# Up-projection weights asked for a chunk ahead, and a transition in which GpSimd keeps the program's order

## The chip, the cores and the metric

The kernel runs on one core of one Trainium2 chip. The metric is the device time of one execution in microseconds (us). A core has five engines that run programs of their own and meet at semaphores: TensorE (PE in the profile; matmuls, results in PSUM), VectorE (DVE), ScalarE (ACT), GpSimd (POOL) and SyncE (SP). SP issues nearly all transfers (DMAs) here, in the order of its program: one that waits for its source holds back those behind it.

## The reference

One decoder layer on x of 1024 tokens by 1024 features, in float32:

```python
h = rmsnorm(x, g_mix) * (1 + sc_m) + sh_m
x = x + gt_m * dsa_mixer(h, ...)            # indexer, top 256 keys, attention on a shared latent
h = rmsnorm(x, g_ffn) * (1 + sc_f) + sh_f
u, v = split(h @ f_w_in, 2)                 # 1024 -> 2 x 2816
u = causal_depthwise_conv(u, f_conv_w, width=3) + f_conv_b
x = x + gt_f * ((gelu(u) * v) @ f_w_out)    # 2816 -> 1024
return rmsnorm(x, g_final)
```

The shifts, scales and gates (`sh`, `sc`, `gt`) are linear in silu(c).

## The kernel before

Every large product is made at float32 accuracy from two parts per operand: a high part (a cast to the matmul format, on ScalarE) and a low part (operand minus its high part, on VectorE or GpSimd). Each 128-deep step is three matmuls of 128x512: high by high, high by low, low by high (`three`). A product with four steps is twelve matmuls.

*The up-projection.* f_w_in is cut into NF = 22 chunks of 128 columns of u and of v. For each chunk `c` the 2x2 block product (u and v by two halves of the tokens) is made with seven products `m0` to `m6` instead of eight, Strassen's way. Their token-side operands (`s3`, `s4`, `b11`, `b22` in `comb`, and `s1`, `s7`, `s6`) are sums of blocks of the normalised tokens `hm`, made once. Their weight-side operands are made for each chunk: two loads, `fw{c}_1` (the v columns) and `fw{c}_0` (the u columns), 512 KB each; for some products a sum of two blocks into `ring` on GpSimd (`prep_sum`); then the high part of `pr{c}_{i}` on ScalarE and its low part on GpSimd, for product 3 on VectorE (`prep_split`). After a product, `after` evicts it: `v` and `u` are put together by VectorE and ScalarE; when m5 is in, ScalarE's `conv` activation starts the convolution, VectorE's two taps follow, then the GELU, and VectorE multiplies with v (`gate`). The result goes to memory (`ga<-conv`); for every second chunk, four sums of two chunks' results (`sa`, `sb`) go there as well.

*Output weights.* The down-projection uses sums of blocks of f_w_out as well. For each pair q of chunks, `w_sums(q)` loads two tiles `wb`, makes four sums and one product with the gate on VectorE and stores them (`wt`). Seven pairs are done in the attention's last part; the remaining four fall into the up-projection, one each in the time of chunks 4, 8, 12 and 16.

*Order.* `LEAD` = 2: when a product is issued, sums are made for products up to two or three ahead and parts for two ahead. Loads follow a plan: (step, chunk) pairs from `LOAD_AT`, where step 7c + `LOAD_AT[j]` asks for `fw{c+1}`. Chunks 0 and 1 are loaded by hand. A scheduler orders each engine's instructions by estimated times, except for engines in the set `in_order`, which keep the program's order.

*The transition.* The loop over r finishes the tokens tile by tile: the output projection `w1` (into `wo`, added to the residual `xr`), the norm (`ss`, `rx`, `rxr`, `xn`), the transposes (`xt`) and `hm` in `w2a`, the parts for `comb` in `w2b`, the pair sums of tiles o and 4 + o in `w2c` (three operations on `hm`), and the parts of `s1`, `s7` and `s6` in `w2d`. Behind the loop, the code for tile 7 is written out by hand together with the first products of chunks 0 and 1, with VectorE, ScalarE and TensorE in program order (`in_order |= set("PAD")`). After the last `w2d` the set is cleared, and the loop over `seq` does the rest.

Of the kernel before, what the change touches and what calls it, by code (L numbers as in the profile page):

```python
# [15 lines left out]
OP = mybir.AluOpType  # L16

T, D, P = 1024, 1024, 128
NT, KD = T // P, D // P
# [45 lines left out]
NW = 'PDDDPPDD'  # L65
W2B_DVE = {(6, 1), (4, 1), (5, 1), (6, 0), (7, 0), (7, 1)}
HM_ACT = (3, 6, 7)
LOAD_AT = (3, 3)
UP_LOW_DVE = ((3,), (3, 6))
D_ORDER = (1, 2, 5, 6, 3, 7, 4)  # L70
D_LOAD, D_SPLIT = 16.0, 7.0
# [5 lines left out]
def body(ctx, tc, a):  # L77
    nc = tc.nc
    in_order = set("PADG")
# [19 lines left out]
    pe, act, dve, pool = [Engine(e, n) for e, n in zip((nc.tensor, nc.scalar, nc.vector, nc.gpsimd), "PADG")]  # L99
# [11 lines left out]
    def slot(shape, dt, name):  # L111
        return slots.tile(shape, dt, name=name, tag="slot")
# [4 lines left out]
    def bank1(name):  # L117
        return bank2(name)[:, :512]
# [4 lines left out]
    def cyc(n, name, bufs, dt=F):  # L123
        return const.tile([P, n], dt, name=name, tag=name, bufs=bufs)

    def split(dst_h, dst_l, src, low):
        act.copy(dst_h, src)
        low.tensor_tensor(dst_l, src, dst_h.bitcast(F), op=OP.subtract)

    def three(out, lh, ll, rh, rl, first, last):  # L130
        pe.matmul(out, lh, rh, start=first, stop=False)
        pe.matmul(out, lh, rl, start=False, stop=False)
        pe.matmul(out, ll, rh, start=False, stop=last)
# [81 lines left out]
    def rstd(ss, n, width, name):  # L215
        t = cyc(width, name, 4)
        dve.tensor_scalar(t, ss, 1.0 / n, EPS, op0=OP.mult, op1=OP.add)
        r = cyc(width, name + "r", 4)
        pool.tensor_tensor(r, t, mhalf.to_broadcast([P, width]), op=OP.pow)
        return r  # L220
# [844 lines left out]
    ost, xn1 = {}, {}  # L1065
# [5 lines left out]
    def w0(t):  # L1071
        if t == 0:
            load_xr(0)
        if t + 1 < NT:
            load_xr(t + 1)
        pt = bank2("ot")
        for k in range(KD):
            pe.transpose(pt[:, k * P:(k + 1) * P], o_sb[t][:, k], ident)
        o_h = slot([P, KD, P], R, "o_h")
        o_l = slot([P, KD, P], R, "o_l")  # L1080
        ost[t] = o_h, o_l
        split(o_h, o_l, pt.rearrange("p (k t) -> p k t", k=KD), dve)

    def w1(t, between=None):

        o_h, o_l = ost[t]
        if between:
            halves = [bank1("wo") for _ in range(2)]
        else:
            ps = bank2("wo")  # L1090
            halves = [ps[:, :512], ps[:, 512:]]
        x1 = x_r[t]
        for j in range(2):
            js = slice(j * 512, (j + 1) * 512)
            for k in range(KD):
                three(halves[j], o_h[:, k], o_l[:, k], wo[k][0][:, js], wo[k][1][:, js], k == 0, k == KD - 1)
            if between:
                dve.tensor_tensor(x1[:, js], halves[j], x1[:, js], op=OP.add)
                if j == 0:
                    between()  # L1100
        if between is None:
            dve.tensor_tensor(x1, ps, x1, op=OP.add)
            nc.sync.dma_start(x1d[t], x1)
            xn1[t] = norm(x1, NW[t])
# [12 lines left out]
    def w2a(t, halves):  # L1117

        hf, o = divmod(t, 4)
        hm[t] = g = slot([P, KD, P], F, f"hm{t}")  # L1120
        for k in range(KD):
            pe.transpose(halves[k // 4][:, k % 4], xn1[t][:, k * P:(k + 1) * P], ident)
        if t in HM_ACT:
            on_dve = 4 if t >= NT - 2 else 0
            if on_dve:
                dve.tensor_tensor(g[:, 0:4], halves[0], bc(ada["a_f"][:, 0:4]), op=OP.mult)
                dve.tensor_tensor(g[:, 0:4], g[:, 0:4], bc(sh_f[:, 0:4]), op=OP.add)
            for k in range(on_dve, KD):
                act.activation(g[:, k], halves[k // 4][:, k % 4], AF.Identity, bias=sh_f[:, k:k + 1], scale=a_f[:, k:k + 1])
        else:  # L1130
            for i in range(2):
                ks = slice(4 * i, 4 * i + 4)
                dve.tensor_tensor(g[:, ks], halves[i], bc(ada["a_f"][:, ks]), op=OP.mult)
            dve.tensor_tensor(g, g, bc(sh_f), op=OP.add)
# [20 lines left out]
    def load_up(c, j):  # L1155
        raw[c, j] = w = slot([P, 2, 4, P], F, f"fw{c}_{j}")
        nc.sync.dma_start(w, a["f_w_in"][c, :, j].rearrange("p (h k m) -> p h k m", h=2, k=4))
# [17 lines left out]
    def prep_sum(c, i):  # L1175
        b0, b1, op, _ = prods[i]
        pair[c, i] = None
        if b1 is None:
            wsum[c, i] = raw[c, b0[0]][:, b0[1]]
        else:  # L1180
            wsum[c, i] = ring[:, nsum[0] % 2]
            nsum[0] += 1
            pool.tensor_tensor(wsum[c, i], raw[c, b0[0]][:, b0[1]], raw[c, b1[0]][:, b1[1]], op=op)

    def prep_split(c, i):
        if (c, i) not in pair:
            prep_sum(c, i)
        pair[c, i] = w = slot([P, 2, 4, P], R, f"pr{c}_{i}")
        split(w[:, 0], w[:, 1], wsum[c, i], dve if (i in UP_LOW_DVE[c >= NF - 2]) else pool)
# [3 lines left out]
    def bank(name):  # L1193
        return banks.tile([P, 512], F, name=name, tag="bk")

    def product(c, i):
        bank_of[c, i] = ps = bank(f"m{i}")
        w = pair[c, i]
        rh, rl = comb[prods[i][3]][:2]
        for k in range(4):  # L1200
            three(ps, w[:, 0, k], w[:, 1, k], rh(k), rl(k), k == 0, k == 3)
# [102 lines left out]
    def w2c(o):  # L1304

        g0, g1 = hm[o], hm[4 + o]
        dve.tensor_tensor(g0[:, 4:8], g0[:, 4:8], g1[:, 4:8], op=OP.add)
        dve.tensor_tensor(g1[:, 0:4], g1[:, 0:4], g0[:, 0:4], op=OP.add)
        dve.tensor_tensor(g0[:, 0:4], g0[:, 0:4], g1[:, 4:8], op=OP.add)
# [3 lines left out]
    def w2d(nm, o, which="hl"):  # L1313

        if nm not in parts:
            parts[nm] = h, lo = [[slot([P, 2, 512], R, f"{nm}{x}{i}") for i in range(2)] for x in "hl"]
            comb[nm] = (lambda k: h[k // 2][:, k % 2]), (lambda k: lo[k // 2][:, k % 2])
        h, lo = parts[nm]
        sl = slice(o * P, (o + 1) * P)
        t, x = {"s1": (o, 0), "s7": (o, 4), "s6": (4 + o, 0)}[nm]  # L1320
        for i in range(2):
            src = hm[t][:, x + 2 * i:x + 2 * i + 2]
            if "h" in which:
                act.copy(h[i][:, :, sl], src)
            if "l" in which:
                dve.tensor_tensor(lo[i][:, :, sl], src, h[i][:, :, sl].bitcast(F), op=OP.subtract)

    for r in range(NT):
        w0(r)
        if r == NT - 2:  # L1330
            load_up(0, 1)
        if r == NT - 1:
            ring = slot([P, 2, 4, P], F, "ring")
            prep_split(0, 0)
            prep_sum(0, 1)
            prep_split(0, 1)
        if r >= 1:
            w1(r - 1)
        if r >= 2:
            w2a(r - 2, [bank1("xt").rearrange("p (k t) -> p k t", k=4) for _ in range(2)])  # L1340
            w2b(r - 2)
        if r >= 6:
            w2c(r - 6)
        for q in range(sum(T_AT[:r]), sum(T_AT[:r + 1])):
            for _ in w_sums(q):
                pass


    in_order |= set("PAD")
    xt6 = bank2("xt").rearrange("p (h k t) -> p h k t", h=2, k=4)  # L1350

    def under_w1():
# [8 lines left out]
    x1 = x_r[NT - 1]  # L1361
    ss = cyc(1, "ss", 4)
    xn1[NT - 1] = slot([P, 1024], F, "xn")
    act.activation(xn1[NT - 1], x1, AF.Square, accum_out=ss)
    prep_split(1, 0)
    w2d("s1", 0, "h")
    rs = rstd(ss, D, 1, "rx")
    w2d("s1", 0, "l")
    dve.tensor_scalar(xn1[NT - 1], x1, rs, None, op0=OP.mult)
    load_up(1, 0)  # L1370
    nc.sync.dma_start(x1d[NT - 1], x1)
    product(0, 0)
    product(0, 1)
    prep_sum(1, 1)
    prep_split(1, 1)
    w2c(2)
    w2d("s1", 1)
    w2d("s1", 2)
    w2a(NT - 1, [bank("xt").rearrange("p (k t) -> p k t", k=4) for _ in range(2)])
    w2b(NT - 1)  # L1380
    product(1, 0)
# [2 lines left out]
    prep_split(0, 2)  # L1384
    prep_split(0, 3)
    product(1, 1)
    w2c(3)
    w2d("s1", 3)
    after(1, 1)
    prep_sum(1, 2)  # L1390
    prep_split(1, 2)
    prep_split(1, 3)
    for o in range(4):
        w2d("s7", o)
    for o in range(4):
        w2d("s6", o)
    in_order.clear()
    seq = [(c, i) for c in range(2) for i in (2, 3)] + [(c, i) for c in range(2) for i in (4, 5, 6)]
    seq += [(c, i) for c in range(2, NF) for i in range(7)]
    prepared = {(c, i) for c in range(2) for i in range(2)} | {(c, i) for c in range(2) for i in (2, 3)}  # L1400
    summed = set(prepared)
    loaded = {(c, j) for c in range(2) for j in range(2)}

# [1 line left out]
    for c in range(NF):  # L1405
        for at_i, j in zip(LOAD_AT, (1, 0)):
            if c + 1 < NF and (c + 1, j) not in loaded:
# [264 lines left out]
```

## Time and profile before

| | us |
|---|---|
| median of 3 runs (lowest, highest) | 1189.42 (1187.14, 1190.0) |
| profiled execution | 1184.61 |
| its span | 1182.8 |
| TensorE busy | 1112.3 (94%) |
| VectorE busy | 902.6 (76%) |
| GpSimd busy | 591.2 (50%) |
| ScalarE busy | 539.1 (46%) |

The span is what the trace covers; 1.8 us of the execution lie around it. The output projection ends at 503 us, the first product of the up-projection starts at 507.57, and the last ends near 966; the down-projection fills the rest. A busy share is an average over stages with different limits; what a stage waits for is read in that stage. Matmuls are pipelined: one of 128x512 is shown with 0.39 us, and the next one starts 0.23 us after it. The granted TensorE clock is given as a share of full speed (1.00 is 2.4 GHz, 0.50 is 1.2 GHz); its mean over the span is 0.976.

### The profile page before, as it was taken

Reading aid. Unit: us, or ns where it says so; the run is one execution under the profiler, and the core shown is the slowest. Engines: PE = TensorE matmul, PEld = TensorE weight load, DVE = VectorE, ACT = ScalarE, POOL = GpSimd, SP = SyncE. Lnnn points to the kernel's source line nnn. Section 1 sums busy time; section 2 is a strip of 40 time slices with the busy share of each in tenths; the row PEclk is TensorE's granted clock in tenths of the full one; section 3 lists DMA queues with packets and bytes.
Section 4 is the critical chain, followed back from the end, with each engine's and each line's share of the span. In section 5 each row is a group of like instructions: output and inputs, shape, how many; then the busy total and the mean of one; then the engine's idle time right before and its main releaser. Section 6 shows DMA issues by size and latency. Waiting matters only on the chain.

```text
span 1182.8 us, 15318 instructions
## 1 busy us (share of the span) xinstructions
PE 1112.3 (94%) x5419; PEld 913.6 (77%) x5419; DVE 902.6 (76%) x1386; ACT 539.1 (46%) x919; POOL 591.2 (50%) x367
## 2 busy tenths in 40 slices
PE   7899999988999999989989989989989999999997
PEld 6787777766777888867768868868868878888886
DVE  6867888798978477788796797778768796555587
ACT  2377876775455323254333333423324355343342
POOL 3453110021244324639979978978979840200353
PEclk8899998999999999989989999989999999999999
DMA  9532102005656686210432443242342449975351
GB/s 366 221 127 90 37 19 72 1 1 160 196 161 195 232 320 231 72 54 27 169 125 80 134 135 124 92 157 90 125 125 97 155 144 369 391 251 179 104 196 71
DMA packets 70505, 174.37 MB, mean 147 GB/s; under 512 B 6512, under 2 KB 10008, under 8 KB 70424
## 3 DMA queue, kind: packets, MB, share of 16 engines
q1 hardware_dynamic: 70280, 173.10, 42.5%
q8 instruction: 42, 0.69, 0.2%
q14 instruction: 39, 0.32, 0.1%
q10 hardware_dynamic: 144, 0.26, 0.1%
HBM read 133.22 MB, written 41.69 MB: 148 GB/s over the span
## 4 chain that ended last, share of the span: by engine, by line
PE 49%; DVE 10%; issue 6%; POOL 4%; DMA 4%; ACT 2%; SPq 0%; POOLq 0%; DVEq 0%; ACTq 0%
PE m L93 21%; PE d L93 18%; PE wo L93 4%; DMA fw<-in_f_w_in 3%; PE o L93 2%; PE l L93 2%; DVE conv L93 2%; POOL pr L93 2%; DVE wb L93 1%; POOL ring L93 1%; PE pt L93 1%; DMA wo<-in_w_o 1%; DVE pr L93 1%; DVE sa L93 1%; DVE hm L93 1%
## 5 line engine op out<-in xcount | busy, mean ns | idle before, releaser
L93 PE MATMUL m<-comb,pr 128*128 128x512 f32 x1056 | 259.1, 403 | 23.5 <-ACT pr L93 13.9
L93 PEld LDWEIGHTS m<-comb,pr 128*128 128x128 f32 x1056 | 204.0, 195 | 73.2 <-ACT pr L93 17.1
L93 POOL TENSOR_TENSOR pr<-ring,pr 128x512 fp32r<-128x512 f32 x108 | 188.3, 1758 | 31.3 <-ACT pr L93 31.1
L93 PE MATMUL d<-ringb,ringa 128*128 128x512 f32 x888 | 202.1, 389 | 0.0
L93 PEld LDWEIGHTS d<-ringb,ringa 128*128 128x128 f32 x888 | 166.7, 188 | 34.5
L93 POOL TENSOR_TENSOR ring<-fw,fw 128x512 f32<-128x512 f32 x66 | 116.1, 1772 | 1.7
L93 POOL TENSOR_TENSOR y<-y,gt_f 128x512 f32<-128x512 f32 x12 | 23.6, 1984 | 156.5 <-DVE y L93 156.5
L93 ACT CAST pr<-ring 128x512 fp32r<-128x512 f32 x110 | 67.1, 618 | 62.8 <-POOL ring L93 62.5
L93 DVE SCALAR_TENSOR_TENSOR conv<-u,small,conv 128x1023 f32<-128x1023 f32 (+1 forms) x44 | 69.3, 1576 | 28.5 <-ACT conv L93 28.4
L93 DVE TENSOR_TENSOR ringa<-da,ringa 128x1024 fp32r<-128x1024 f32 (+1 forms) x40 | 49.0, 1226 | 51.2 <-ACT ringa L93 51.1
L93 DVE TENSOR_TENSOR u<-m,u 128x512 f32<-128x512 f32 x66 | 45.4, 687 | 51.5 <-PE m L93 34.7
L93 POOL TENSOR_TENSOR ring<-fw 128x512 f32<-128x512 f32 x44 | 63.5, 1446 | 34.8 <-DMA fw<-in_f_w_in 34.8
L93 ACT CAST ringa<-da 128x1024 fp32r<-128x1024 f32 (+1 forms) x40 | 39.5, 987 | 90.5 <-PE d L93 78.8
L93 PEld LDWEIGHTS o<-vv,ptb 128*128 128x128 f32 x528 | 64.1, 192 | 9.7 <-issue 3.8
L93 ACT ACTIVATE lg<-lg,mx 128x128 f32<-128x128 f32 (+6 forms) x64 | 49.5, 774 | 45.4 <-DVE mx L93 45.3
L93 PE MATMUL o<-vv,ptb 128*128 128x128 f32 x528 | 67.1, 276 | 2.8 <-DVE o L93 2.8
L93 PE MATMUL l<-kt,q 128*128 128x512 f32 (+3 forms) x160 | 65.4, 523 | 4.0 <-ACT ptb L93 2.2
L93 PE MATMUL m<-s1h,pr 128*128 128x512 f32 x176 | 58.2, 391 | 1.9 <-POOL pr L93 1.9
L93 PE MATMUL m<-s7h,pr 128*128 128x512 f32 x176 | 58.1, 391 | 1.1 <-ACT pr L93 0.7
L93 PE MATMUL m<-s6h,pr 128*128 128x512 f32 x176 | 57.8, 389 | 0.0
L93 ACT CAST pr<-fw 128x512 fp32r<-128x512 f32 x44 | 27.2, 618 | 61.6 <-DMA fw<-in_f_w_in 61.6
L93 ACT ACTIVATE conv<-u,small 128x1024 f32<-128x1024 f32 x22 | 27.4, 1245 | 59.1 <-DVE u L93 59.1
(292 smaller groups left out, 2561.6 us busy)
## 6 DMA issues: line engine op xcount, KB each, us to landing
fw<-in_f_w_in SPq DMA_DIRECT2D x44, 512.0 KB, 5.1
da<-ga SPq DMA_DIRECT2D x35, 512.0 KB, 6.9
ada<-in_ada_w SPq DMA_DIRECT2D x32, 512.0 KB, 4.0
wb<-in_f_w_out SPq DMA_DIRECT2D x22, 512.0 KB, 6.6
wt<-wb SPq DMA_DIRECT2D x44, 256.0 KB, 2.3
db<-wt SPq DMA_DIRECT2D x20, 512.0 KB, 9.3
ga<-conv SPq DMA_DIRECT2D x33, 256.0 KB, 2.2
db<-in_f_w_out SPq DMA_DIRECT2D x15, 512.0 KB, 6.6
```

Source lines behind the costliest of these rows:

```text
L93: r = f(*args, **kw)
```

## The change

Four edits.

1. The plan asks for `fw{c+1}_1` at step 7c - 1 and for `fw{c+1}_0` at 7c, for chunk 2 and on, instead of both at 7c + 3.
2. In the loop over the tiles the pair sums `w2c` are made for o = 0 only; those for o = 1 move behind tile 7's norm, and those for o = 2 further back.
3. GpSimd is in program order too in the transition.
4. The transition's code is in another order: the scaling of tile 7 (`xn`) directly behind its norm factor; the parts of `s1` later; the weight parts of products (1,2) and (1,3) earlier; those of (0,4) and (0,5) now written in the transition, around the parts of `s7`.

```diff
-LOAD_AT = (3, 3)
+LOAD_AT = (-1, 0)
...
-        if r >= 6:
-            w2c(r - 6)
+        if r == NT - 2:
+            w2c(0)
...
-    in_order |= set("PAD")
+    in_order |= set("PADG")
...
     act.activation(xn1[NT - 1], x1, AF.Square, accum_out=ss)
+    rs = rstd(ss, D, 1, "rx")
+    dve.tensor_scalar(xn1[NT - 1], x1, rs, None, op0=OP.mult)
     prep_split(1, 0)
-    w2d("s1", 0, "h")
-    rs = rstd(ss, D, 1, "rx")
-    w2d("s1", 0, "l")
-    dve.tensor_scalar(xn1[NT - 1], x1, rs, None, op0=OP.mult)
+    w2c(1)
+    w2d("s1", 0)
     load_up(1, 0)
...
     prep_split(1, 1)
-    w2c(2)
-    w2d("s1", 1)
-    w2d("s1", 2)
     w2a(NT - 1, ...)
...
     product(1, 1)
+    prep_sum(1, 2)
+    prep_split(1, 2)
+    w2c(2)
+    prep_split(1, 3)
+    for o in range(1, 3):
+        w2d("s1", o)
     w2c(3)
     w2d("s1", 3)
     after(1, 1)
-    prep_sum(1, 2)
-    prep_split(1, 2)
-    prep_split(1, 3)
+    prep_sum(0, 4)
+    prep_split(0, 4)
     for o in range(4):
         w2d("s7", o)
+    prep_sum(0, 5)
+    prep_split(0, 5)
     for o in range(4):
         w2d("s6", o)
```

Three places show what moves. First SP's program around the loads of chunk 5 (`fw5_1`, `fw5_0`); `sa`, `sb` and `wb` are the tiles named above. Before:

```order
L1286 DMA wt6_3_4289<-wb1_5814 128x512
L1265 DMA ga5_0_4256<-sa_5860 128x512
L1265 DMA ga7_0_4268<-sb_5861 128x512
L1157 DMA fw5_1_5889<-in_f_w_in 128x1024
L1157 DMA fw5_0_5891<-in_f_w_in 128x1024
L1265 DMA ga6_0_4262<-sa_5860 128x512
```

After:

```order
L1157 DMA fw4_0_5675<-in_f_w_in 128x1024
L1244 DMA ga1_0_4232<-conv_5650 128x512
L1157 DMA fw5_1_5796<-in_f_w_in 128x1024
L1157 DMA fw5_0_5815<-in_f_w_in 128x1024
L1273 DMA wb0_5817<-in_f_w_out 128x1024
L1273 DMA wb1_5818<-in_f_w_out 128x1024
L1286 DMA wt5_3_4283<-wb0_5817 128x512
L1246 DMA ga2_0_4238<-conv_5790 128x512
```

The two loads stood behind a store that waits for VectorE's `sb`; they now stand one store behind `fw4_0` and in front of `wb`.

Second, VectorE's program between tile 6's `hm` and tile 7's `xn`. Before, with the pair sum of `hm1` and `hm5` in front:

```order
L93 TENSOR_TENSOR diff_5057<-hm5_5044 128x512
L93 TENSOR_TENSOR hm1_4639<-hm1_4639,hm5_5044 128x512
L93 TENSOR_TENSOR hm5_5044<-hm5_5044,hm1_4639 128x512
L93 TENSOR_TENSOR comb_4299<-diff_5057,comb_4299 128x4x128
L93 TENSOR_TENSOR hm1_4639<-hm1_4639,hm5_5044 128x512
L93 TENSOR_TENSOR xr7_4863<-wo_5066,xr7_4863 128x512
L93 TENSOR_TENSOR hm6_5097<-xt_5065,a_f_4222 128x512
L93 TENSOR_TENSOR hm6_5097<-hm6_5097,sh_f0_3734 128x512
L93 TENSOR_TENSOR diff_5113<-hm6_5097 128x512
L93 TENSOR_TENSOR comb_4299<-hm6_5097,comb_4299 128x4x128
L93 TENSOR_TENSOR comb_4299<-diff_5113,comb_4299 128x4x128
L93 TENSOR_TENSOR xr7_4863<-wo_5067,xr7_4863 128x512
```

After:

```order
L93 TENSOR_TENSOR diff_5057<-hm5_5044 128x512
L93 TENSOR_TENSOR comb_4299<-diff_5057,comb_4299 128x4x128
L93 TENSOR_TENSOR xr7_4863<-wo_5063,xr7_4863 128x512
L93 TENSOR_TENSOR hm6_5094<-xt_5062,a_f_4222 128x512
L93 TENSOR_TENSOR hm6_5094<-hm6_5094,sh_f0_3734 128x512
L93 TENSOR_TENSOR diff_5110<-hm6_5094 128x512
L93 TENSOR_TENSOR comb_4299<-hm6_5094,comb_4299 128x4x128
L93 TENSOR_TENSOR comb_4299<-diff_5110,comb_4299 128x4x128
L93 TENSOR_TENSOR xr7_4863<-wo_5064,xr7_4863 128x512
L93 TENSOR_SCALAR rx_5147<-ss_5144 128x1
L93 TENSOR_SCALAR xn_5145<-xr7_4863,rxr_5149 128x1024
L93 TENSOR_TENSOR hm1_4639<-hm1_4639,hm5_5044 128x512
```

The three `hm1`/`hm5` sums have left the stretch in front of the second `xr7`, and `xn` follows on `rx` at once (the two parts of `s1l` that stood between them before are beyond the piece).

Third, GpSimd's program from tile 6's last `comb` part on. Before:

```order
L93 TENSOR_TENSOR ring_4975<-fw1_1_5093 128x512
L93 TENSOR_TENSOR ring_4975<-fw0_0_5095 128x512
L93 TENSOR_TENSOR rxr_5161<-rx_5159,mhalf_76 128x1
L93 TENSOR_TENSOR pr1_0_5150<-fw1_1_5093,pr1_0_5150 128x512
L93 TENSOR_TENSOR pr1_1_5196<-ring_4975,pr1_1_5196 128x512
L93 TENSOR_TENSOR ring_4975<-fw1_0_5166 128x512
L93 TENSOR_TENSOR pr0_2_5250<-ring_4975,pr0_2_5250 128x512
L93 TENSOR_TENSOR ring_4975<-fw0_0_5095,fw0_1_4878 128x512
L93 TENSOR_TENSOR pr1_2_5280<-ring_4975,pr1_2_5280 128x512
```

After:

```order
L93 TENSOR_TENSOR rxr_5149<-rx_5147,mhalf_76 128x1
L93 TENSOR_TENSOR pr1_0_5152<-fw1_1_5090,pr1_0_5152 128x512
L93 TENSOR_TENSOR ring_4975<-fw1_1_5090 128x512
L93 TENSOR_TENSOR pr1_1_5196<-ring_4975,pr1_1_5196 128x512
L93 TENSOR_TENSOR ring_4975<-fw0_0_5092 128x512
L93 TENSOR_TENSOR pr0_2_5239<-ring_4975,pr0_2_5239 128x512
L93 TENSOR_TENSOR ring_4975<-fw1_0_5166 128x512
L93 TENSOR_TENSOR pr1_2_5259<-ring_4975,pr1_2_5259 128x512
L93 TENSOR_TENSOR ring_4975<-fw0_0_5092,fw0_1_4878 128x512
```

The two block sums that stood in front of `rxr` now stand behind the low part of `pr1_0`, and each block sum directly in front of the low part that it feeds or one ahead of it.

## Rows read from the trace of the kernel before

**Rows 1.** Page's groups (busy, mean ns, idle before, releaser) and issues (KB, landing us)

```profile
L93 ACT CAST pr<-fw 128x512 fp32r<-128x512 f32 x44 | 27.2, 618 | 61.6 <-DMA fw<-in_f_w_in 61.6
...
fw<-in_f_w_in SPq DMA_DIRECT2D x44, 512.0 KB, 5.1
```

**Rows 2.** Stretches: length, busy us of PE, PEld, DVE, ACT, POOL; clock

```profile
600.00:640.00 40.00, 36.08 (x147) 28.88 (x146) 29.51 (x31) 13.28 (x21) 30.69 (x20) 0.91 0.37 119
640.00:680.00 40.00, 40.00 (x179) 33.10 (x178) 31.91 (x31) 14.76 (x23) 37.70 (x24) 1.00 0.37 125
```

**Rows 3.** Waits from 560 to 966: total us, times, longest

```profile
ACT pr L93 <- DMA fw<-in_f_w_in: 61.6, 15, 9.7
...
PE m L93 <- ACT pr L93: 13.9, 5, 3.8
```

**Rows 4.** TensorE's timeline, first event: start, duration, operation, idle before

```profile
593.63 10.59 PE L93 MATMUL m<-comb,pr 128*128 128x512 f32 x46
...
615.51 1.22 PE L93 MATMUL m<-comb,pr 128*128 128x512 f32 x2 [3.13 <-ACT pr L93]
617.51 12.75 PE L93 MATMUL m<-comb,pr 128*128 128x512 f32 x46 [0.79 <-POOL pr L93]
```

**Rows 5.** Stretches of the event, columns as in rows 2

```profile
593.20:612.40 19.20, 19.18 (x85) 15.57 (x83) 19.20 (x16) 5.33 (x9) 14.84 (x8) 1.00 0.37 111
...
615.00:621.80 6.80, 5.50 (x12) 3.91 (x13) 5.37 (x6) 4.29 (x6) 6.80 (x4) 0.50 0.33 128
```

**Rows 6.** Timeline of SP's DMA issues around the event

```profile
582.63 0.86 SPq L1157 DMA_DIRECT2D fw<-in_f_w_in  x2
...
609.16 0.32 SPq L1265 DMA_DIRECT2D ga<-sb  x1
609.57 0.88 SPq L1157 DMA_DIRECT2D fw<-in_f_w_in  x2
```

**Rows 7.** Timeline of ScalarE around the event

```profile
615.96 1.24 ACT L93 ACTIVATE conv<-u,small 128x1024 f32<-128x1024 f32 x1 [0.50 <-DVE u L93]
617.10 0.60 ACT L93 CAST pr<-ring 128x512 fp32r<-128x512 f32 x1
```

**Rows 8.** Timeline of VectorE around the event

```profile
607.36 1.78 DVE L93 TENSOR_TENSOR sb<-conv 128x512 f32<-128x512 f32 x1
609.06 0.68 DVE L93 TENSOR_TENSOR wb<-wb 128x512 f32<-128x512 f32 x1
...
615.24 0.68 DVE L93 TENSOR_TENSOR u<-m,u 128x512 f32<-128x512 f32 x1
```

**Rows 9.** Timeline of GpSimd around the event

```profile
605.15 3.44 POOL L93 TENSOR_TENSOR pr<-ring,pr 128x512 fp32r<-128x512 f32 x2
614.95 1.28 POOL L93 TENSOR_TENSOR ring<-fw 128x512 f32<-128x512 f32 x1 [6.37 <-DMA fw<-in_f_w_in]
```

**Rows 10.** Timeline of TensorE in the transition

```profile
507.57 8.08 PE L93 MATMUL m<-comb,pr 128*128 128x512 f32 x24 [4.24 <-DVE xr L93]
```

**Rows 11.** Stretch behind the transition's pause, columns as in rows 2

```profile
505.80:512.60 6.80, 5.03 (x12) 4.00 (x13) 4.89 (x7) 3.70 (x9) 3.22 (x3) 0.50 0.48 155
```

**Rows 12.** Timeline of VectorE in the transition

```profile
497.25 2.38 DVE L93 TENSOR_TENSOR hm<-hm,hm 128x512 f32<-128x512 f32 x2
499.56 1.77 DVE L93 TENSOR_TENSOR comb<-diff,comb 128x512 fp32r<-128x512 f32 x1
...
506.74 0.68 DVE L93 TENSOR_TENSOR xr<-wo,xr 128x512 f32<-128x512 f32 x1
```

**Rows 13.** Timeline of GpSimd in the transition

```profile
497.32 3.46 POOL L93 TENSOR_TENSOR ring<-fw 128x512 f32<-128x512 f32 x2 [0.54 <-DMA fw<-in_f_w_in]
...
550.59 1.28 POOL L93 TENSOR_TENSOR pr<-fw,pr 128x512 fp32r<-128x512 f32 x1
```

**Rows 14.** Timeline of ScalarE at the up-projection's end

```profile
942.18 0.62 ACT L93 CAST pr<-fw 128x512 fp32r<-128x512 f32 x1 [3.25 <-DMA fw<-in_f_w_in]
```

**Rows 15.** Timeline of TensorE at the up-projection's end

```profile
957.85 0.72 PE L93 MATMUL m<-s1h,pr 128*128 128x512 f32 x2 [0.78 <-POOL pr L93]
```

More of the change, by code (lines that the diff above doesn't have):

```diff
@@ L1399, in body @@
     seq += [(c, i) for c in range(2, NF) for i in range(7)]
-    prepared = {(c, i) for c in range(2) for i in range(2)} | {(c, i) for c in range(2) for i in (2, 3)}
+    prepared = {(c, i) for c in range(2) for i in range(2)} | {(c, i) for c in range(2) for i in (2, 3)} | {(0, 4), (0, 5)}
     summed = set(prepared)
```

## The prediction

> **What bounds the kernel now.** I read the page's list of costliest groups first and look in it for idle time with a transfer as its end: ScalarE's casts of `pr`, where they read `fw` directly, waited 61.6 us for the weight load [rows 1]. So the place is the up-projection. A table by 40 us stretches [rows 2] then shows that the loss isn't spread out: 640 to 680 has TensorE busy for 40.00 of 40 us, 600 to 640 only for 36.08, at a granted clock of 0.91. GpSimd is at 37.70 of 40 in the undisturbed stretch, so it has some 2 us to spare there and no more. The waits of the whole up-projection [rows 3] give ScalarE's wait for `fw` as 15 pieces with a longest of 9.7, and TensorE's wait for the casts as five pieces with 13.9 in all. Four of the five are one event repeated, in chunks 4, 8, 12 and 16, the chunks in whose time the pair sums of the output weights (`wb`) run on VectorE.
>
> The first event, step by step. TensorE normally issues a matmul every 0.227 us: 46 take 10.59, the last one alone 0.39 [rows 4]. It stops at 615.51 - 3.13 = 612.38, runs two matmuls in 1.22 instead of 0.62, stops again for 0.79, and takes 12.75 for the next 46 instead of 10.59 [rows 4], because the granted clock is 0.50 from 615.0 to 621.8 [rows 5], the lower of its two levels (1.2 against 2.4 GHz), behind the pause. The loss is 3.13 + 0.60 + 0.79 + 2.16 = 6.7 us, and four such events are 27 us. The immediate cause is in the SP queue: `fw5` goes out at 609.57, right behind a store of `sb` that left at 609.16, when VectorE had written it [rows 6], and GpSimd gets to work on it at 614.95 [rows 9].
>
> But there is a second lateness behind the first. The second product of chunk 5 needs ScalarE's cast at 617.10, and in ScalarE's order the convolution's first activation stands in front of it, at 615.96, which waited for VectorE's `u<-m` [rows 7]. That one started at 615.24 [rows 8], although its product had left TensorE by 610.1 (ten matmuls of 0.227 lie between its last one and 612.38). VectorE was simply late: it was busy for 19.20 of the 19.20 us from 593.2 to 612.4 [rows 5]. Beside a working GpSimd, its operations with both inputs in SBUF follow at 1.70 us (607.36 to 609.06); once GpSimd is idle, one takes 0.68 [rows 8] and the eleven instructions from 609.06 to 615.24 follow at 0.6. And GpSimd was idle exactly then, from 605.15 + 3.44 = 608.59 to 614.95, because it too had no `fw5` [rows 9]. The late load thus let VectorE catch up.
>
> **The change part by part.** *Loads a chunk ahead.* In the new SP order `fw5` stands one store behind the place at which `fw4` went out at 582.63 [rows 6]. At 5.1 us from issue to landing [rows 1] it lands near 590, ahead of the cast's turn at about 606. It is moved past stores and past the two loads of `wb`, which now stand behind it: with one load after another they are there by 593 or 594, and VectorE's busy stretch with their first reading begins at 593.2 with other work [rows 5]. So the load's wait goes entirely, in all four events. What is late next: TensorE runs the first product of chunk 5 at once, to 612.38 + 12 x 0.227 = 615.1, and then needs the cast behind the convolution. GpSimd now has three operations ready at 608.6 (the low part of that product, two block sums), 1.72 us each beside VectorE (3.44 for two [rows 9]), so until 613.8. In these 5.2 us VectorE passes about 2.6 SBUF operations at 1.70 instead of 0.60, 2.9 us lost; the four it still has are `sa`, `sb` and two of `wb`, in another order than before but the same ones. `u<-m` ends at 615.24 + 0.68 + 2.9 = 618.8, and the cast ends as far behind it as before (617.10 + 0.60 - 615.92 = 1.78), at 620.6. TensorE's pause is 620.6 - 615.1 = 5.5 us, one pause instead of two. The clock fell in each of the four old events, and I assume it falls in this one too: it costs 2.76 of the first old event (0.60 + 2.16); here part of the slow time lies inside the pause, and I take 1.7. Together 7.2 against 6.7: +0.5 an event, +2 us for four. Bounds: VectorE as early as before (cast ends 617.7, pause 2.6, clock nothing) gives -4.1 an event, -16; a pause of 5.5, 0.7 of waiting for the low part and a clock at half speed over as much work as takes 6.8 us (3.4) gives 9.6, +2.9 an event, +12. I take the middle piece because its rows (1.70, 1.72) are from the same few microseconds.
>
> The Trainium skill (SBUF — State Buffer, section "Who interferes with whom") speaks against this part more strongly: the port pair that VectorE shares with GpSimd is an exclusive lock, and the loser waits for the other's whole instruction. By that rule a VectorE operation with two SBUF inputs would come every 0.60 + 1.28 = 1.88 us beside GpSimd, not 1.70, some 0.5 us more per event and 2 us over four. The trace has the slowing but at the smaller size (1.70), and the measurement decides.
>
> *The transition between attention and up-projection.* TensorE waits 4.24 us before the first product at 507.57 [rows 10], for the second half of the residual sum `xr` on VectorE at 506.74 [rows 12], and then runs at a clock of 0.50, 5.03 us busy from 505.8 to 512.6 [rows 11]. In VectorE's new order three `hm` sums go out of the chain in front of `xr`; two of them and their follower cost 497.25 to 499.56, 2.3 us, the third 0.6 [rows 12]. The `comb<-diff` at 499.56 took 1.77 beside GpSimd's two block sums (497.32, 3.46 long [rows 13]); these now stand behind GpSimd's `rxr`, so it should take 0.69, another 1.0. That is 3.9 of which 0.7 is lost again because TensorE itself ends the output projection only at 503.3 (507.57 - 4.24): `xr` at 503.5, first product at 504.35, 3.2 us earlier, pause 1.0, and probably no fall of the clock, worth 5.03 / 2 = 2.5 more. Not all of that arrives. GpSimd in program order has twelve operations between the low part of product (0,4) and that of (2,0). TensorE is at (0,4) at about 504.35 + 8 x 2.73 + 1.0 for the transposes = 527, GpSimd starts there near 528, and at 1.7 each it ends at 548.4, against 550.59 + 1.28 = 551.87 before [rows 13]. I take 3.5 us of gain. Bounds: 5.7 (start and clock in full) and -2 (GpSimd's fixed order holds a low part behind a block sum twice, 1.3 to 1.7 each, and the start's gain only just pays for one). The two block sums that GpSimd did while it waited for tile 7's norm now lie between the first low parts, when TensorE still has whole products in hand. The pair sums that leave the front are hidden behind the same products; if that cover goes, they cost the 2.9 us again.
>
> *The end.* The last chunk's load is late as well, for GpSimd more than TensorE: the cast waited 3.25 [rows 14] and TensorE 0.78 later [rows 15]. Asked for a chunk earlier, this gives 0 to 1.9; I take 0.9. In the chunks without `wb` TensorE had no pause [rows 2], and earlier loads change nothing there. TensorE's new order in a chunk puts the last `u` product 0.45 us later (two matmuls of the next product go in front); outside the four events the 2.3 us in 40 that GpSimd has to spare [rows 2] hide it; without them it is 0.45 a chunk.
>
> *Sum.* +2.0 - 3.5 - 0.9 = -2.4 us. It is worked out from the profiled execution (1184.61 us, span 1182.8), which is 4.8 below the median of the runs; I take the difference over: 1189.42 - 2.4 = 1187.0.
>
> **The rivals.** *The wait was the load's alone* (27 us come back): 1189.4 - 27 - 4.4 = 1158. For it: 61.6 us of waits with one name. Against it: `u<-m` at 615.24 with its product done five microseconds before [rows 8]. 0.07. *VectorE keeps up*: it passes its SBUF operations before GpSimd's three, the pause is 2.6 and the clock costs 0.7, 3.3 instead of 6.7: -13.6 - 4.4, that is 1171. For it: GpSimd's margin is small and its three operations could fall later. Against: nothing else on GpSimd waits then. 0.16. *The longer pause costs the clock in full*, the slower side: 5.5 in one piece, and behind it half speed for 3.4 to 6.8 us of the following products in each of the four chunks, +10, with the transition and end as forecast: 1189.4 + 10 - 4.4 = 1195. It decides from a pause as long as that in front of the first product, 4.24, behind which the clock stayed at 0.50 until 512.6 [rows 10, 11]; against it, the old events' pauses of 3 us had falls too, so the difference may be small. 0.17. *The transition gives nothing*, since GpSimd's fixed order makes TensorE wait in place of VectorE: +2 instead of -3.5, 1192.5. 0.10. The forecast itself has 0.50.
>
> **How the numbers follow.** About 0.3% (3.6 us) is what a measurement of this kernel can tell from no change. The forecast's own range is 1182 to 1192; of its 0.50 I put 0.18 below 1185.8, 0.29 within, 0.03 above 1193. Faster: 0.18 + 0.07 + 0.16 = 0.41, and a little from the transition at its upper bound, 0.42. Slower: 0.17 + 0.03 and half of the transition's rival, 0.25. The rest, 0.33, is no change. The range reaches to VectorE keeping up (1171, and 3 below) and to the full clock cost (1195, and 2 above).
>
> **What would show it.** In the changed profile: ScalarE's wait for `fw` small in all chunks; in its place, in chunks 4, 8, 12 and 16, ScalarE's `conv` waiting for VectorE's `u`, VectorE at 1.70 us a step up to about 614, `u<-m` ending near 619, and a TensorE pause near 5.5 us before the second product of the next chunk with a clock of 0.50 behind it. In the transition: first product near 504.4, clock 1.00 there, first low part of chunk 2 near 548. A pause under 3 us in the four events would make the forecast wrong on the fast side; a wait of TensorE for GpSimd between 505 and 550 of more than 5 us in all, or a clock fall of 6.8 us in each event, on the slow side.

## The result

The changed kernel takes 1196.55 us (median of 6 runs, 1194.96 to 1201.02) against 1189.47 before: the ratio is 1.0073, with a 95% interval of 1.0049 to 1.0096. It is slower, by 6 to 11 us; 1187.0 was forecast, on the other side. The profiled execution took 1195.84 us (span 1194.1).

First, what waits for a transfer. In the page of the changed kernel the groups read (busy, mean ns | idle before, releaser):

```profile
L93 POOL TENSOR_TENSOR pr<-ring,pr 128x512 fp32r<-128x512 f32 x108 | 187.6, 1753 | 75.4 <-ACT pr L93 75.4
...
L93 ACT ACTIVATE conv<-u,small 128x1024 f32<-128x1024 f32 x22 | 27.3, 1243 | 145.1 <-DVE u L93 145.1
```

The 61.6 us of ScalarE's casts behind `fw` [rows 1] are gone from the list. In their place ScalarE's convolution waits 145.1 us for VectorE's `u` (59.1 before), and GpSimd waits 75.4 for ScalarE's casts (31.1 before). The table of stretches (columns as in [rows 2]) shows that TensorE has not been helped:

```profile
500.00:560.00 60.00, 48.61 (x196) 36.42 (x195) 53.48 (x65) 27.25 (x59) 32.63 (x23) 0.94 0.13 44
...
600.00:640.00 40.00, 34.28 (x140) 27.76 (x139) 34.60 (x29) 13.46 (x22) 32.17 (x19) 0.91 0.37 124
640.00:680.00 40.00, 40.00 (x178) 33.13 (x177) 30.86 (x31) 14.64 (x22) 35.95 (x23) 1.00 0.31 106
```

600 to 640 has 34.28 us of TensorE work, 36.08 before; 640 to 680 is full in both. And the stretch of the transition, 500 to 560, is at 48.61 of 60. Before, it had 52.98:

```profile
500.00:560.00 60.00, 52.98 (x219) 41.06 (x218) 50.62 (x70) 30.83 (x63) 37.17 (x25) 0.94 0.12 40
```

TensorE's waits in the changed kernel, there and in the first event, one by one:

```profile
504.44 5.71 PE L93 MATMUL m<-comb,pr 128*128 128x512 f32 x24 [1.08 <-DVE xr L93]
...
517.69 1.25 PE L93 MATMUL m<-comb,pr 128*128 128x512 f32 x4 [1.21 <-ACT pr L93]
...
539.41 0.79 PE L93 MATMUL m<-s7l,pr 128*128 128x512 f32 x1 [4.93 <-DVE s7l L93]
...
552.84 0.50 PE L93 MATMUL m<-s7h,pr 128*128 128x512 f32 x1 [2.00 <-ACT pr L93]
...
627.57 11.14 PE L93 MATMUL m<-comb,pr 128*128 128x512 f32 x36 [5.72 <-ACT pr L93]
```

The start of the up-projection is where the prediction had it, 504.44, with a wait of 1.08 instead of 4.24 [rows 10]. But 35 us later TensorE waits 4.93 for `s7l` (the low parts of `s7`, `s7h` being the high ones), which VectorE makes, and then 2.00 for a cast. Within the first of these waits the granted clock falls, as it did within the 4.24 before [rows 11]:

```profile
537.70:544.50 6.80, 5.09 (x12) 3.79 (x12) 6.80 (x8) 0.49 (x1) 5.57 (x4) 0.50 0.00 0
```

By the end of chunk 5's first product, TensorE's stop is at 627.57 - 5.72 = 621.85; the same point would have come at 615.1 before (612.38 and twelve matmuls [rows 4]). So 6.7 us are lost by there, ahead of the first event. The event itself is the forecast one: one pause, 5.72 us in all four chunks. These are readings of two single executions: with the output projection ending at 503.36 and 503.32, the last product ends at 977.54, before at 966.33. That is 11.2 us, while the medians are 7.1 apart, mostly because the profiled execution before lies 4.8 below its median.

VectorE in the transition, the changed kernel first, then the kernel before (rows that were not shown ahead of the prediction):

```profile
506.33 1.77 DVE L93 TENSOR_SCALAR xn<-xr,rxr 128x1024 f32<-128x1024 f32 x1 [0.66 <-POOL rxr L93]
...
519.47 4.08 DVE L93 TENSOR_TENSOR hm<-hm,hm 128x512 f32<-128x512 f32 x3
...
530.62 10.15 DVE L93 TENSOR_TENSOR s7l<-hm,s7h 128x256 fp32r<-128x256 f32 x8
540.70 4.92 DVE L93 TENSOR_TENSOR s6l<-hm,s6h 128x256 fp32r<-128x256 f32 x8
```

```profile
529.71 3.86 DVE L93 TENSOR_TENSOR s7l<-hm,s7h 128x256 fp32r<-128x256 f32 x8
533.49 2.77 DVE L93 TENSOR_TENSOR s6l<-hm,s6h 128x256 fp32r<-128x256 f32 x8
```

The sixteen low parts of `s7` and `s6` start 0.9 us later than before and take 15.0 us instead of 6.5. GpSimd shows why, in the changed kernel:

```profile
530.36 1.28 POOL L93 TENSOR_TENSOR pr<-ring,pr 128x512 fp32r<-128x512 f32 x1 [5.65 <-ACT pr L93]
531.60 2.92 POOL L93 TENSOR_TENSOR ring<-fw,fw 128x512 f32<-128x512 f32 x2
534.48 1.45 POOL L93 TENSOR_TENSOR pr<-ring,pr 128x512 fp32r<-128x512 f32 x1
536.01 1.33 POOL L93 TENSOR_TENSOR ring<-fw,fw 128x512 f32<-128x512 f32 x1
537.75 2.74 POOL L93 TENSOR_TENSOR pr<-ring,pr 128x512 fp32r<-128x512 f32 x2 [0.41 <-ACT pr L93]
540.45 2.87 POOL L93 TENSOR_TENSOR ring<-fw,fw 128x512 f32<-128x512 f32 x2
552.86 3.12 POOL L93 TENSOR_TENSOR pr<-ring,pr 128x512 fp32r<-128x512 f32 x2 [9.54 <-ACT pr L93]
555.95 2.27 POOL L93 TENSOR_TENSOR pr<-fw,pr 128x512 fp32r<-128x512 f32 x1
```

From 530.36 to 543.3 it works almost without pause on the weight parts from product (0,4) on (chunk 0, product 4), and VectorE's operations beside it come every 1.27 us (10.15 for eight). Row by row, one of VectorE's goes with one of GpSimd's and ends 0.28 us behind it, nine of nine, as here:

```profile
531.60 1.49 POOL L93 TENSOR_TENSOR ring<-fw,fw 128x512 f32<-128x512 f32 x1
531.85 1.52 DVE L93 TENSOR_TENSOR s7l<-hm,s7h 128x256 fp32r<-128x256 f32 x1
```

Behind 543.3 the last six come every 0.34 us. In the kernel before, GpSimd was idle from 530.93 to 534.38, and when it came back it was GpSimd that was held: its operation took 3.00 us instead of 1.28, while VectorE's parts of `s6` went on at 0.34:

```profile
529.31 1.62 POOL L93 TENSOR_TENSOR ring<-fw,fw 128x512 f32<-128x512 f32 x1
534.38 3.00 POOL L93 TENSOR_TENSOR pr<-ring,pr 128x512 fp32r<-128x512 f32 x1 [3.45 <-ACT pr L93]
```

What decides which of the two is held, these runs don't show. In the changed kernel VectorE is 9 us late with `u` (545.54, 536.17 before), the first convolution is late on ScalarE, the casts behind it too, and GpSimd waits 9.54 us for them (row 552.86): the 2.00 us of TensorE at 552.84.

### The profile page after: what moved, and what is told of

It is laid out like the page before. It is cut to its first block, busy times and chain, and to the rows that moved or that the text cites. A ratio compares the mean times of both kernels' runs of the same rounds, so it can differ in the third digit from the quotient of the medians.

```text
span 1194.1 us, 15333 instructions
## 1 busy us (share of the span) xinstructions
PE 1116.0 (93%) x5419; PEld 917.6 (77%) x5419; DVE 917.5 (77%) x1386; ACT 537.0 (45%) x919; POOL 591.8 (50%) x367
## 4 chain that ended last, share of the span: by engine, by line
PE 48%; DVE 12%; issue 8%; POOL 4%; ACT 2%; DMA 1%; POOLq 0%; DVEq 0%; ACTq 0%; SPq 0%
PE m L93 20%; PE d L93 18%; PE wo L93 4%; PE o L93 2%; DVE conv L93 2%; PE l L93 2%; POOL pr L93 2%; DVE wb L93 1%; DVE u L93 1%; DVE sb L93 1%; DVE sa L93 1%; PE pt L93 1%; POOL ring L93 1%; DVE hm L93 1%; DVE pr L93 1%
## 5 line engine op out<-in xcount | busy, mean ns | idle before, releaser
L93 POOL TENSOR_TENSOR pr<-ring,pr 128x512 fp32r<-128x512 f32 x108 | 187.6, 1753 | 75.4 <-ACT pr L93 75.4
L93 ACT ACTIVATE conv<-u,small 128x1024 f32<-128x1024 f32 x22 | 27.3, 1243 | 145.1 <-DVE u L93 145.1
L93 POOL TENSOR_TENSOR mn<-near,score 128x1024 f32<-128x1024 f32 x8 | 19.9, 2493 | 67.8 <-ACT jk L93 26.5
```

The costliest lines, as they stand in the source:

```text
L93: r = f(*args, **kw)
```

## The experiments

All twelve were timed beside the kernel before on the same chip; ratios are to it, with 95% intervals.

**Loads alone.**

```diff
-LOAD_AT = (3, 3)
+LOAD_AT = (-1, 0)
```

> The kernel before with the first edit alone (weights asked for a chunk ahead). Theory (the edit swaps one wait for another: VectorE's backlog makes ScalarE's convolution late, and the next product's cast stands behind it): four TensorE pauses of 5.7 us with 6.8 us of half clock behind each, ScalarE's wait for fw gone, its wait for u long; about 5 us slower than before, 1192 to 1197. Rival (the events cost the same as before and the whole loss is the transition's): no change, 1188 to 1191. Second rival (two edits only lose together): faster than before.

1190.28 us, 1.0005 (0.9991 to 1.0019): no change. The first theory has the mechanism (TensorE's waits from 560 to 966 in this run):

```profile
PE m L93 <- ACT pr L93: 22.9, 4, 5.7
```

Four waits, the longest 5.7, as in the changed kernel, and no cast waits for `fw`. Its price was too high: the time is the rival's. So the exchange of waits costs 0.7 us (-1.1 to 2.3), and most of the loss is elsewhere.

**Transition alone.** The changed kernel with `LOAD_AT = (3, 3)`.

> The changed kernel with the old load plan, so the transition's edits alone. Theory (VectorE is the transition's limit, and GpSimd working beside it halves its pace): the pause for s7l of about 5 us stays, the up-projection's fifth chunk starts 6 to 7 us later than before, the four old events as before; 6 to 7 us slower than before, 1194 to 1198. Rival (the transition is fine and the loss comes from the loads): 1185 to 1189, 3 us faster.

1196.6 us, 1.0068 (1.0049 to 1.0087). By the medians it is 7.0 us: as far as the runs can tell, the whole loss is here, with the same waits:

```profile
538.40 0.80 PE L93 MATMUL m<-s7l,pr 128*128 128x512 f32 x1 [4.88 <-DVE s7l L93]
...
551.83 0.51 PE L93 MATMUL m<-s7h,pr 128*128 128x512 f32 x1 [1.99 <-ACT pr L93]
```

**GpSimd free in the transition.**

```diff
-    in_order |= set("PADG")
+    in_order |= set("PAD")
```

> The changed kernel with GpSimd left to the scheduler in the transition (third edit undone). Theory (VectorE's parts of s7 and s6 run at half pace because GpSimd works beside them on the parts of products (0,4) and (0,5)): only two block sums move in front of the norm, GpSimd still works beside s7l, the pause of 5 us stays: 1194 to 1198. Rival (the fixed order itself is what costs): 1186 to 1190.

1195.77 us, 1.006 (1.0039 to 1.0081), as the theory has it. The fixed order of GpSimd is not the cause: left to the scheduler, it still works beside VectorE, and `s7l` and `s6l` take 14 us together (TensorE's wait comes in two pieces here, 2.77 for `s7l` and 2.40 for `s6l`):

```profile
531.87 6.92 DVE L93 TENSOR_TENSOR s7l<-hm,s7h 128x256 fp32r<-128x256 f32 x8
538.71 7.07 DVE L93 TENSOR_TENSOR s6l<-hm,s6h 128x256 fp32r<-128x256 f32 x8
```

**Parts of (0,4) and (0,5) later.**

```diff
-    prep_sum(0, 4)
-    prep_split(0, 4)
     for o in range(4):
         w2d("s7", o)
-    prep_sum(0, 5)
-    prep_split(0, 5)
     for o in range(4):
         w2d("s6", o)
```

> The changed kernel without the fourth edit's last piece: the weight parts of products (0,4) and (0,5) are not written between those of s7 and s6 but left to the loop behind. ScalarE then casts s7 and s6 first and GpSimd has nothing to do meanwhile. Theory (contention with GpSimd): the 16 operations s7l and s6l take 7 to 9 us instead of 15, the pause for s7l goes, 1186 to 1191. Rival (VectorE simply has too much in front of s7l, whatever GpSimd does): s7l as late as in the changed kernel, 1194 to 1198.

1191.02 us, 1.001 (0.9991 to 1.003): about 5 of the 7 us are back. VectorE's rows, GpSimd's and TensorE's:

```profile
532.84 2.76 DVE L93 TENSOR_TENSOR s7l<-hm,s7h 128x256 fp32r<-128x256 f32 x8
535.52 2.76 DVE L93 TENSOR_TENSOR s6l<-hm,s6h 128x256 fp32r<-128x256 f32 x8
```

```profile
538.17 2.52 POOL L93 TENSOR_TENSOR pr<-ring,pr 128x512 fp32r<-128x512 f32 x2 [11.02 <-ACT pr L93]
```

```profile
538.14 0.80 PE L93 MATMUL m<-s1h,pr 128*128 128x512 f32 x1 [5.53 <-ACT pr L93]
```

With GpSimd idle for 11 us, the same sixteen operations take 5.5 us, though they start no earlier (27.0 us behind the first product at 505.80; 26.2 in the changed kernel). The wait for `s7l` is gone; another of 5.53 has come, for the cast of product (0,4), which now stands behind sixteen casts of `s7` and `s6` on ScalarE. That VectorE's pace beside GpSimd is the cause is shown by this run; that the transition has no slack on ScalarE either is its second finding.

**Front of the transition alone.** The kernel before, with `w2c(1)` behind the norm and `xn` right behind `rs`.

> The kernel before with the front of the transition alone: the pair sums of hm1 and hm5 behind tile 7's norm and xn right behind its factor; all else as before. Theory (the start's 3 us are real, and what eats them in the changed kernel is the later part): first product 3 us earlier, 1186 to 1188. Rival (VectorE's work is only put off and delays tile 7's parts or s7l by as much): 1189 to 1191.

1188.4 us, 0.9988 (0.9968 to 1.0007): not told from no change, so it is the rival's. TensorE's rows say where the 2.6 us of the shorter first wait go:

```profile
509.93 5.72 PE L93 MATMUL m<-comb,pr 128*128 128x512 f32 x24 [1.61 <-DVE xr L93]
...
525.47 1.73 PE L93 MATMUL m<-comb,pr 128*128 128x512 f32 x4 [3.49 <-ACT pr L93]
```

The wait in front of the first product is 1.61 instead of 4.24, and 15 us later comes one of 3.49 for a cast that stands behind tile 7's work on ScalarE; `xn` ends 4.5 us sooner behind the output projection, but the pair sums now stand in front of tile 7's `hm` on VectorE, and ScalarE's cast of it comes 14.2 us behind the end of the output projection, 14.9 before.

**Sums of the output weights one chunk later.** The kernel before, with its late loads.

```diff
-T_UP = (60.0, 71.7, 8.0)
+T_UP = (77.9, 71.7, 8.0)
```

> The kernel before with its old load plan; only the four late sets of output-weight sums (wb) are put one chunk later, into chunks that have no sa and sb sums. Theory (VectorE's backlog is the root of both the late load, through the store in front of it in SP's queue, and the late cast): fw5 goes out about 7 us earlier, VectorE is in time, the events shrink to 0 to 2 us each; 20 to 28 us faster, 1161 to 1169. Rival (the load's place in the queue is a limit of its own): events lose 1 to 2 us of their 7, 1181 to 1186.

1177.21 us, 0.9894 (0.9875 to 0.9914): 12 us faster, between the two. The casts still wait for `fw`, nearly as long in all, in more and shorter pieces, and TensorE still stops once in each of the four events, for 2.3 to 2.8 us; the last row is the cast that ends the first of these stops:

```profile
ACT pr L93 <- DMA fw<-in_f_w_in: 59.7, 19, 5.8
...
PE m L93 <- ACT pr L93: 11.1, 6, 2.8
...
636.28 0.62 ACT L93 CAST pr<-fw 128x512 fp32r<-128x512 f32 x1 [5.84 <-DMA fw<-in_f_w_in]
```

So with the sums moved, what is left of the events hangs on the load. (With the sums where they were, the load's place alone gave nothing.)

**Both: loads ahead, sums one chunk later.** The old transition.

> The kernel before with both the loads a chunk ahead and the wb sums one chunk later; the transition is the old one. Theory (with VectorE unburdened, the early load is worth at most what the late one still costs): no pause above 1 us in chunks 4 to 20, 25 to 29 us faster than before, 1160 to 1165, and within 3 us of the run with the sums moved alone. Rival (the backlog moves along with the sums, into chunks 5, 9, 13 and 17): four pauses there of 3 to 6 us, 1180 to 1195.

1164.91 us, 0.9785 (0.9772 to 0.9799), 25 us faster. That this is within 3 us of the run before is wrong, it is 12 below. The stretches and TensorE's waits from 560 to 950:

```profile
560.00:600.00 40.00, 39.70 (x175) 32.38 (x174) 32.08 (x32) 15.04 (x23) 37.84 (x24) 1.00 0.35 117
600.00:640.00 40.00, 39.33 (x172) 31.69 (x171) 36.82 (x33) 14.52 (x22) 37.13 (x23) 1.00 0.44 151
...
680.00:720.00 40.00, 39.33 (x172) 31.60 (x171) 36.82 (x33) 14.53 (x22) 37.13 (x23) 1.00 0.44 152
```

```profile
PE m L93 <- POOL pr L93: 3.2, 10, 0.7
PE m L93 <- ACT pr L93: 1.7, 4, 0.4
```

No wait is above 0.7 us, and the granted clock stays at 1.00. VectorE is busy 36.8 of 40 us in the stretches with the moved sums, and TensorE has no pause from it. The two gains hang on each other: the earlier loads are worth nothing with the backlog in place, and 12 us without it.

**The same with the front of the transition.**

> The front of the transition together with the loads a chunk ahead and the wb sums one chunk later. Theory (three separate places, so their gains add): 2 to 3 us below the run with loads and sums moved, 1161 to 1163. Rival (no gain from the front): 1164 to 1166.

1164.37 us, 0.9793 (0.9764 to 0.9822): the rival, no gain told from the run before. These two are the fastest found.

**ScalarE's order in the event.** In the next runs the first activation of the convolution is issued with the taps, and so stands behind the next chunk's casts of products 1 and 2.

```diff
-            act.activation(s, u, AF.Identity, bias=convb[:, c:c + 1], scale=cw[2])
-
             def taps():
+                act.activation(s, u, AF.Identity, bias=convb[:, c:c + 1], scale=cw[2])
```

With the loads ahead and the sums where they were:

> The kernel before with the loads a chunk ahead and, on ScalarE, the convolution's first activation moved behind the next chunk's casts of products 1 and 2 (it is issued together with the taps). The wb sums stay in the chunks with sa and sb, so VectorE is as late as in the changed kernel. Theory (what stops TensorE is ScalarE's order, the cast behind a convolution that waits for VectorE): the pauses of 5.7 us shrink to under 3, ScalarE's casts come in time; 14 to 26 us faster than before, 1163 to 1175. Rival (VectorE's lateness stops TensorE by another way, the eviction or its own low part of product 3): pauses stay, 1186 to 1192.

1179.07 us, 0.99 (0.9877 to 0.9924): the pauses of 5.7 are gone. ScalarE's rows in the event, and TensorE's waits from 560 to 966:

```profile
617.31 0.62 ACT L93 CAST pr<-ring 128x512 fp32r<-128x512 f32 x1 [5.65 <-POOL ring L93]
619.10 0.62 ACT L93 CAST pr<-ring 128x512 fp32r<-128x512 f32 x1 [1.18 <-POOL ring L93]
620.54 1.24 ACT L93 ACTIVATE conv<-u,small 128x1024 f32<-128x1024 f32 x1 [0.81 <-DVE u L93]
```

```profile
PE m L93 <- POOL pr L93: 8.3, 14, 0.7
PE m L93 <- ACT pr L93: 3.5, 5, 1.0
```

The casts come at 617.31 and 619.10, ahead of a convolution that still waits for VectorE at 620.54, and the longest wait is 1.0. That ScalarE's order carried VectorE's lateness to TensorE is shown. The gain, 11 us, is below the range expected: a wait of 0.7 us for a low part of GpSimd's comes in every second chunk, and from the last product's end to the span's it is 219.1 us instead of 216.5. Why these two come is not shown.

With the old late loads:

> The kernel before with its late loads, and ScalarE's convolution behind the two casts, as in the run before this one. Theory (two waits one behind the other, of which the load's comes first): ScalarE still waits 9 us for fw in four chunks, the events lose at most 1 us each, 1185 to 1190. Rival (ScalarE's order alone is the cause): 1163 to 1175.

1192.54 us, 1.0016 (1.0002 to 1.0031). Above both ranges, though no gain, as the theory has it. The trace is against the theory's reason: the longest wait of a cast for `fw` is 3.7 us here, not 9, and many small waits have come instead: TensorE's for GpSimd and ScalarE are 19.8 us in 33 pieces (19.4 in 11 before), none above 1.4, and the end takes 220.7 us. That the load's wait came first of the two is not shown by this run, and stays open.

With loads ahead, sums moved and the convolution behind, and then the front of the transition too:

> Loads a chunk ahead, wb sums one chunk later, and the convolution behind the two casts; transition as before. Theory (the 1.9 us that each shifted event still costs come by the same order on ScalarE): these go, 5 to 8 us below the run with loads and sums moved, 1157 to 1161. Rival (the rest is GpSimd's own pace): 1163 to 1166.

> The run before this one with the front of the transition as well (pair sums behind the norm, xn at once). Theory (the front's gain is eaten by a wait for a cast in the transition, as seen): within 1.5 us of the run before this one. Rival (it adds): 2 to 3 us less.

1178.05 us, 0.9904 (0.9865 to 0.9942), and 1178.45 us, 0.9887 (0.9863 to 0.9911). Both expectations for the first are wrong: the new order on ScalarE costs some 13 us (0.9904 against 0.9785) where there is no pause left to remove. The traces say where and not why: from the output projection's end to the last product's it is 450.7 us instead of 441.6, with TensorE's waits for GpSimd at 7.2 us in 13 pieces from 560 to 966, and from there to the end 219.1 again instead of 216.5. The second agrees with the theory, nothing added.

## Why the prediction was wrong

*The transition (forecast -3.5, bounds -5.7 to +2).* This is the step that failed. Its first half held: first product forecast at 504.35, measured 504.44, a wait of 1.0 against 1.08, and no fall of the clock there. What failed is "GpSimd in program order has twelve operations between the low part of product (0,4) and that of (2,0) ... it ends at 548.4". I took GpSimd's pace as what decides the rest, and did not lay VectorE's queue beside it. VectorE had the sums put off from the front and sixteen low parts of `s7` and `s6`, and GpSimd, kept busy from 530 to 543 by the parts moved there, more than halved the pace of those: 15.0 us instead of 6.5. The low part of (2,0) ended at 558.2, not for GpSimd's pace: it stood idle for 9.54 us in front of it, waiting for casts that stood, on ScalarE, behind a convolution that waited for VectorE. The sign I had set for this failure, TensorE waiting for GpSimd, stayed at 0.62 us between 505 and 550; the waits were for VectorE and ScalarE. The transition alone is 1.0068 of before, 7.0 us by the medians where -3.5 was forecast; taking the parts of (0,4) and (0,5) away gives back about 5 us. The rival I had written for it blamed GpSimd's fixed order, at +2; the order is not the cause, and its price was a third of the loss. The same contention is in my term for the events, just ahead of it; I had not applied it to the low parts here.

*The sums put off are hidden behind the first products.* Wrong as well, though it isn't what cost the time: in the run with the front alone they show up as a wait of 3.49 and eat its gain; in the changed kernel the waits there are 1.21 and 0.66, and the sums push back VectorE's later work (`s7l` starts 26.2 us behind the first product, 22.1 before).

*The events (forecast +2.0).* Right in mechanism: the load's wait goes, VectorE's backlog takes its place through ScalarE's order, pause forecast 5.5, measured 5.72. VectorE's rows in the first event, to be laid beside [rows 8]:

```profile
612.79 1.77 DVE L93 TENSOR_TENSOR sb<-conv 128x512 f32<-128x512 f32 x1
614.49 0.68 DVE L93 TENSOR_TENSOR v<-m,v 128x512 f32<-128x512 f32 x1
...
616.19 1.77 DVE L93 TENSOR_TENSOR sa<-sa,conv 128x512 f32<-128x512 f32 x1
617.88 1.77 DVE L93 TENSOR_TENSOR wb<-wb 128x512 f32<-128x512 f32 x1
...
625.05 0.68 DVE L93 TENSOR_TENSOR u<-m,u 128x512 f32<-128x512 f32 x1
```

The operations with both inputs in SBUF mostly come at 1.70 until GpSimd stops at 620.8, and all at 0.6 behind; `u<-m` ends 625.73 - 621.85 = 3.9 us behind TensorE's stop, 3.7 forecast. The term of the clock was mis-sized: the clock falls within each of the four pauses and is at 0.50 for 6.83 us (a sign that I had set for the slow side), as here (columns as in [rows 2], to be laid beside [rows 5]):

```profile
626.50:633.30 6.80, 5.73 (x14) 4.47 (x15) 6.25 (x5) 3.12 (x5) 5.70 (x3) 0.50 0.30 107
```

The 36 matmuls behind the four pauses take 11.14, 11.33, 9.88 and 10.67 us, where 36 at 0.227 (the last alone 0.39) would be 8.3: 9.7 us lost in all, where four times 1.7 was forecast. The first event thus costs 5.72 + 2.8 = 8.5 us, not 7.2. In these two traces that puts the four events and the end some 4.5 us above before (the 11.2 less the 6.7). The runs don't bear it out in full: loads alone measured +0.7 (-1.1 to 2.3) for this and the next term together, forecast +1.1, and 4.8 of the difference between the traces is the profiled execution before lying below its median. The naive rival (27 us back) is out; the rival in which VectorE keeps up came true only once the sums were moved.

*The end (forecast -0.9).* A wait for GpSimd of 0.72 us is still there where 0.78 was [rows 15]; nearly nothing came of it.

*The sum.* With the transition at its measured price (7.0 by the run with it alone) in place of -3.5 it would have been 1187.0 + 3.5 + 7.0, about 1197.5; 1196.55 came.

The rule of the Trainium skill that I weighed (SBUF — State Buffer, "Who interferes with whom": the port pair that VectorE and GpSimd share is an exclusive lock) could have told more than I took from it. I only weighed whether it would shift 1.70 to 1.88. What follows from it for a small operation is the point here: one that has to wait for a whole instruction of the other engine loses as much as a large one. The trace agrees: a half-size operation, 0.34 us alone, took 1.27 beside GpSimd, nine of nine ended 0.28 us behind an operation of GpSimd's, and it was slowed 3.7 times where the full size was slowed 2.8 times (0.60 to 1.70). A fixed share of bandwidth would slow both alike.

## What to carry to other kernels

Before a load is moved ahead, look at what the stalled engine's neighbours did with the stall: here VectorE caught up in it, and without it the same time was lost to the next wait in line; the gain came only when the backlog was moved as well (25 us for both, 12 for one, none for the other). When work is moved to start earlier on GpSimd, price what it does to VectorE beside it, operation by operation, and small operations first. On an engine that works in order, one instruction that waits for a late engine holds back work that could have gone ahead.

## What the runs showed of the hardware

VectorE's operations on two SBUF operands beside a busy GpSimd came at about one per operation of GpSimd's, in the two sizes seen here: 128x512 from 0.60 to 1.70 us a step (GpSimd's took 1.73), 128x256 from 0.34 to 1.27 (GpSimd's took 1.28 to 1.49). Sixteen of the small ones are 5.5 us alone and took 15.0 with GpSimd at work until 543.3. VectorE isn't always the one held: in the kernel before, five of the small ones ran at 0.34 while an operation of GpSimd's took 3.00 us instead of 1.28.

The lower clock lasted 6.83 us in each of the changed kernel's four events (pauses of 5.72 us). In the profile of the loads alone, with pauses of 5.72 to 5.74, it lasted 6.83 in three and 3.41 in one. In the old events, with two pauses (3.1 to 3.8 and 0.8 to 1.3), it was 3.41 us in two and 6.83 in two before, and 6.83 in all four in the profile of the transition alone. So in these traces the length of the slow time does not follow from the pause. Shorter pauses had falls too: with the sums alone moved, the pauses of 2.82, 2.56 and 2.30 us had one of 3.41 us each, the one of 2.64 none.
